# Hybrid decoder trunk on one core: another order of the twelve projection chunks, and the recurrence's side work one or two steps later

## The chip, the cores and the metric

The kernel runs on one core of a Trainium2 chip. The metric is the device time of one execution in microseconds, the median of several runs.

## What is computed

Two layers; each takes a residual `x` of 256 tokens by 1024 and adds the output projection of two mixers that share one input projection:

```python
def hybrid_layer(x, ...):
    h = rms_norm(x, norm_g)
    z = h @ w_in
    (rg_x, rg_gate, q, k_c, v_c, k_s, v_s, k_w, v_w, nsa_gate, br_gate) = jnp.split(z, cuts, axis=-1)
    y_a = rg_lru(causal_depthwise_conv(rg_x, conv_w, conv_b), ...)
    y_a = y_a * jax.nn.silu(rg_gate)
    y_b = nsa(q, k_c, v_c, k_s, v_s, k_w, v_w, br_gate, ...)
    y_b = y_b * jax.nn.silu(nsa_gate)
    return x + jnp.concatenate([y_a, y_b], axis=-1) @ w_out
def rg_lru(x, ...):
    r, i = sigmoid(x @ w_r + b_r), sigmoid(x @ w_i + b_i)      # eight blocks of 64
    a = exp(-8 r softplus(-lam))
    u = sqrt(1 - a * a) * (i * x)
    return associative_scan(h[t] = a[t] * h[t-1] + u[t])
```

`nsa` is an attention of eight query heads on two key heads with three branches: compressed blocks (a softmax over 15 compressed keys), selected blocks and a window; with 256 tokens the last two see the same causal keys.

## The kernel before

**Products.** Every weight is split into a high part `wh` and a remainder `wl` (float32 values of reduced width), and so is the normalised input (`hh`, `hl`). Each product is made of three matmuls, `mm3`, lines 172 to 175, on TensorE: L173, L174 and L175. The remainder of a weight chunk, L168, is made by VectorE; the high part by ScalarE (L165) or, for chunks marked `dma`, by a casting transfer that POOL issues (L156). The raw weights come over SP's queue (L148).

**Steps.** A layer is a list of steps; each has one weight chunk, and `plan` (from line 769) hangs side work on it. Eight steps project q and keys, five the compressed keys and the values. Then come **the twelve chunk steps that the change concerns**, numbered 0 to 11, each of 24 products of 256 columns (`fm`, L406) into a bank called `fm`, and eight steps of output projection (`out_proj`), numbered 12 and on in the plan. The chunks are of three kinds: `x0` to `x3` are the inputs of the recurrence (128 channels each), `g0` to `g3` its output gate, `n0` to `n3` the gate of the attention. What follows a chunk is

- `rg_x` (L640) behind an `x` chunk: one scaling L646 on VectorE into one of two `xpad` buffers, the convolution's first tap L647 on ScalarE, its other three L649 on VectorE; the result is `cx`;
- `silu_gate` (L540) behind every second `g` or `n` chunk, for the pair: L542 and L545 on VectorE, L544 on ScalarE; the result is `sgr` or `sgn`.

**Side work.** The table `SL` (line 53) says before which step each piece is issued: `gates` for `rg_gates` (L652: two gate products L657 on TensorE, then L660, L661, L663, L664 on ScalarE; for every second one L667, L670 on VectorE and L669 on ScalarE), `sqrt` for the root (L673, with a load of another activation table before it, and L674), `scan` for the recurrence's four scans (L678), `rout` for its output (L682, then L560 and L561 into `yy`, the operand of the output projection). The rest of the table is the attention: `qk` transposes queries and keys (L369, L378; `kd`, `kl`, `qs`: L373 to L383), `att` the scores of a head pair and a token half (L579 to L581 into one of three `s` banks, the maximum L584 or L586 on VectorE, the exponential L592 and the scaling L605 on ScalarE), `turn` their transposes (L618, copied by L83), `cmp` the compressed keys (L466, L470, L475 and so on), `cs` and `cpt` the compressed softmax (L509, L512, L515, L517 to L531, L536, and the copy `pct`, L83), `aout` the attention's output products (L628 to L634), which need `pct` and, right behind them on VectorE (L636), the gate `sgn`.

**What sets the order.** The steps are written out one after the other (lines 828 to 845). The tile framework then orders the instructions of each engine by its own estimate of the times and puts in the semaphores. On the chip each engine works its list off in that order: an instruction that waits holds up all that is behind it on the same engine. The weights are prefetched: loads run up to six steps ahead, in four raw buffers, casts up to five, and remainders one to three.

Of the kernel before, what the change touches and what calls it, by code (L numbers as in the profile page):

```python
# [38 lines left out]
for _n, _w in (("g", 8), ("cw", 16), ("cb", 4), ("br", 4), ("bi", 4), ("lam", 4)):  # L39
# [10 lines left out]
PRB = 6  # L50

K = dict(scale="A", ev1="A", hid="A", pct="A")
SL = dict(qk=(0, 2), order=("x0", "x1", "x2", "x3", "n0", "n1", "g0", "g1", "g2", "g3", "n2", "n3"),
          cmp=(2, 3, 4), att=(1, 3, 3, 4, 6, 7, 10, 11), turn=(2, 4, 5, 6, 8, 10,
          12, 13), cs=(5, 5), cpt=6, aout=(6, 7, 12, 15), gates=(2, 3, 4, 5), tab=6, sqrt=5,
          scan=8, rout=(9, 11))

# [12 lines left out]
def hybrid_trunk_kernel(ctx: ExitStack, tc: tile.TileContext, vx, wc, wt, wv, wf, wo, w1, w2, pe,  # L72
# [183 lines left out]
    def layer(l, prev):  # L256
# [4 lines left out]
        def step(chunk, run, after=None, before=(), middle=()):  # L261
            steps.append((chunk, run, after, before, middle))
# [502 lines left out]
        step(Chunk(wv[l, 0, :, 6:], 2, 280), R(tm2, 6, 2), v_out)  # L765
        order = [(o[0], int(o[1])) for o in SL["order"]]
        base = {"x": 0, "g": 4, "n": 8}
# [3 lines left out]
        def at(n, f, *a, mid=False):  # L771
            plan[n][1 if mid else 0].append(F(f, *a))

        at(1, cmp_hid)
        at(SL["qk"][0], qk_transpose, 0)
        at(SL["qk"][1], qk_transpose, 1)
        for n, f in zip(SL["cmp"], (cmp_act, cmp_kv, cmp_kt)):
            at(n, f)
        for q in range(8):
            i, t = divmod(q, 2)  # L780
            n = SL["att"][q]
            at(n, att_scores, i, t)
            at(n, att_coef, i, t, mid=True)
        at(SL["cs"][0], cmp_scores)
        at(SL["cpt"], cmp_pt)
# [168 lines left out]
```

## Time and profile before

| | us |
|---|---|
| median of three runs | 253.13 (252.58 to 253.38) |
| profiled execution, its own time | 252.82 |
| its span | 251.0 |
| twelve chunk steps of layer 0, from the first `fm` product to the output projection | 37.8 to 102 |
| the same of layer 1 | 158 to 222 |

| engine | busy us | share of the span |
|---|---|---|
| TensorE, matmuls | 243.0 | 97% |
| TensorE, weight loads | 222.2 | 88% |
| VectorE | 195.8 | 78% |
| ScalarE | 164.5 | 66% |
| POOL | 40.1 | 16% |

The busy share is an average over a span with several stages. Matmuls are pipelined, each shows some 0.28 us and the next begins 0.12 us after it, so a busy TensorE is not one at its peak. An instruction's length on VectorE and ScalarE overlaps the next by about 0.1 us; the pace of a queue is read from one start to the next.

### The profile page before, as it was taken

How to read it: one execution, taken by the hardware profiler on the slowest of the kernel's cores; microseconds unless marked ns; L12 is line 12 of the kernel's file. 1: busy time of each engine (PE TensorE's matmuls, PEld its weight loads, DVE VectorE, ACT ScalarE, POOL GpSimd, SP SyncE). 2: the span in 40 equal slices, each digit the busy share in tenths (PEclk: the TensorE clock that was granted, in tenths of full speed). 3: DMA queues.
4: the chain of work that ended last, by engine and by line, in shares of the span. 5: the costliest groups of instructions: out<-in, count | busy, mean ns of one | idle time of the engine just before them, and what ended most of it. 6: DMA issues, size and time to landing. Idle time of an engine off the chain costs nothing.

```text
span 251.0 us, 5217 instructions
## 1 busy us (share of the span) xinstructions
PE 243.0 (97%) x1958; PEld 222.2 (88%) x1958; DVE 195.8 (78%) x386; ACT 164.5 (66%) x419; POOL 40.1 (16%) x65
## 2 busy tenths in 40 slices
PE   7999998999999999999999999998999999999994
PEld 3989997977899798999999999996889879989993
DVE  4898798879999997654995569688999998765422
ACT  5966419799999967622873553849999996670000
POOL 0034460001811011000001044100100001010000
PEclk9999999999999999999999999999999999999999
DMA  6987999856699688562569878475249858833022
GB/s 211 371 289 226 318 413 407 265 168 202 195 322 403 184 266 293 174 202 72 167 207 347 312 236 263 159 230 187 93 167 347 317 177 268 271 127 84 3 84 84
DMA packets 17593, 57.17 MB, mean 228 GB/s; under 512 B 2208, under 2 KB 3360, under 8 KB 17056
## 3 DMA queue, kind: packets, MB, share of 16 engines
q1 hardware_dynamic: 12816, 39.86, 46.4%
q0 software_dynamic: 4608, 16.78, 20.9%
q8 instruction: 15, 0.25, 0.4%
q10 hardware_dynamic: 144, 0.20, 0.2%
q14 instruction: 10, 0.08, 0.1%
HBM read 55.78 MB, written 1.05 MB: 226 GB/s over the span
## 4 chain that ended last, share of the span: by engine, by line
PE 59%; DVE 19%; ACT 12%; DMA 4%; issue 2%; POOL 1%; SPq 0%; DVEq 0%; ACTq 0%
PE fm L173 11%; PE fm L175 10%; PE fm L174 10%; DVE wl L168 6%; PE s L174 4%; PE s L175 4%; PE s L173 4%; ACT pr L592 3%; PE m L628 3%; PE pp L618 3%; DMA raw<-in_wt_dram 2%; DMA raw<-in_wf_dram 2%; DVE cx L649 2%; POOL st L179 1%; DVE sm L584 1%
## 5 line engine op out<-in xcount | busy, mean ns | idle before, releaser
L168 DVE TENSOR_TENSOR wl<-raw,wh 128x1024 fp32r<-128x1024 f32 (+4 forms) x67 | 74.4, 1117 | 7.9 <-PE pp L174 3.0
L173 PE MATMUL fm<-hh,wh 128*128 128x256 f32 x192 | 56.9, 296 | 0.2
L174 PE MATMUL fm<-hl,wh 128*128 128x256 f32 x192 | 55.0, 287 | 0.0
L175 PE MATMUL fm<-hh,wl 128*128 128x256 f32 x192 | 54.5, 284 | 0.5 <-DVE wl L168 0.5
L165 ACT CAST wh<-raw 128x768 fp32r<-128x768 f32 (+4 forms) x35 | 30.8, 883 | 28.6 <-DMA raw<-in_wc_dram 7.6
L173 PEld LDWEIGHTS fm<-hh,wh 128*128 128x128 f32 x192 | 36.7, 191 | 2.1 <-issue 1.2
L175 PEld LDWEIGHTS fm<-hh,wl 128*128 128x128 f32 x192 | 36.7, 191 | 1.2 <-DVE wl L168 0.8
L174 PEld LDWEIGHTS fm<-hl,wh 128*128 128x128 f32 x192 | 36.7, 191 | 0.5 <-issue 0.4
L592 ACT ACTIVATE pr<-s,sm 128x128 f32<-128x128 f32 (+1 forms) x64 | 26.0, 417 | 9.4 <-DVE sm L586 6.0
L173 PE MATMUL fm<-yy,wh 128*128 128x256 f32 x96 | 27.4, 285 | 0.0
L175 PE MATMUL fm<-yy,wl 128*128 128x256 f32 x96 | 26.8, 279 | 0.0
L174 PE MATMUL fm<-yy,wh 128*128 128x256 f32 x96 | 26.8, 279 | 0.0
L605 ACT ACTIVATE pr<-pr,sm 128x128 f32<-128x128 f32 (+1 forms) x64 | 23.7, 455 | 1.8 <-DVE sm L598 1.8
L173 PEld LDWEIGHTS fm<-yy,wh 128*128 128x128 f32 x96 | 18.0, 188 | 1.5 <-DVE sm L597 0.8
L156 POOL DMA_DIRECT2D wh<-in_wo_dram x16 | 8.5, 530 | 66.2 <-PE fm L175 29.1
L174 PEld LDWEIGHTS fm<-yy,wh 128*128 128x128 f32 x96 | 18.1, 188 | 0.0
L175 PEld LDWEIGHTS fm<-yy,wl 128*128 128x128 f32 x96 | 18.0, 188 | 0.0
L174 PE MATMUL s<-wl,hh 128*128 128x384 f32 x48 | 16.5, 344 | 0.3 <-DVE wl L168 0.3
L723 DVE TENSOR_TENSOR head<-head,fm 128x512 f32<-128x512 f32 x11 | 7.5, 686 | 11.5 <-PE fm L175 11.5
L156 POOL DMA_DIRECT2D wh<-in_wf_dram x16 | 9.0, 565 | 46.2 <-PE fm L175 24.4
L175 PE MATMUL s<-wh,hl 128*128 128x384 f32 x48 | 16.2, 337 | 0.0
L173 PE MATMUL s<-wh,hh 128*128 128x384 f32 x48 | 15.6, 353 | 0.3 <-ACT wh L165 0.3
(205 smaller groups left out, 615.0 us busy)
## 6 DMA issues: line engine op xcount, KB each, us to landing
raw<-in_wf_dram SPq DMA_DIRECT2D x24, 512.0 KB, 4.5
wh<-in_wf_dram POOLq DMA_DIRECT2D x16, 512.0 KB, 4.8
raw<-in_wo_dram SPq DMA_DIRECT2D x16, 512.0 KB, 5.0
wh<-in_wo_dram POOLq DMA_DIRECT2D x16, 512.0 KB, 4.5
raw<-in_wt_dram SPq DMA_DIRECT2D x15, 384.0 KB, 3.9
yy<-in_w_dram SPq DMA_DIRECT2D x4, 1024.0 KB, 7.4
raw<-in_wc_dram SPq DMA_DIRECT2D x4, 512.0 KB, 5.2
raw<-in_wv_dram SPq DMA_DIRECT2D x4, 420.0 KB, 4.9
```

The source lines that it names most:

```text
L156: G.dma_start(self.wh, self.src)
L165: A.copy(hi[:, c], self.raw[:, c])
L168: V.tensor_tensor(lo[:, c], self.raw[:, c], hi[:, c].bitcast(F32), op=ALU.subtract)
L173: T.matmul(o, lh, rh, start=start, stop=False)
L174: T.matmul(o, lh, rl, start=False, stop=False)
L175: T.matmul(o, ll, rh, start=False, stop=stop)
L592: A.activation(pr[g][:, b], ov[:, b], AF.Exp, bias=sm[:, 0, 2 * g + b:2 * g + b + 1], accum_out=sm[:, 1, 2 * g + b:2 * g + b + 1])
L605: A.activation(pr[g][:, b], pr[g][:, b], AF.Copy, scale=sc_)
L618: T.transpose(pp[:, (2 * g + b) * P:(2 * g + b + 1) * P], pr[g][:, b, c * P:(c + 1) * P], ident)
L628: T.matmul(yb[g * HD:(g + 1) * HD, :S], L.vv[:, 0, b, g * HD:(g + 1) * HD], pt[:, g, b, 0:2].rearrange("p a s -> p (a s)"), start=(b == 0) ...
L649: V.scalar_tensor_tensor(cx[:, j], xp[:, 1 + k:1 + k + S], v(l, "cw", 4 * k + j), cx[:, j], op0=ALU.mult, op1=ALU.add)
L723: V.tensor_tensor(x_sb[:, m], x_sb[:, m], os_[0].rearrange("p (a s) -> p a s", a=2), op=ALU.add)
```

## The change

The chunks `n0` and `n1` go from steps 4 and 5 to steps 0 and 1; the four `x` chunks from steps 0 to 3 to steps 2 to 5; `g0` to `g3`, `n2` and `n3` stay. The gate products of the recurrence go from steps 2, 3, 4, 5 to steps 4, 5, 6, 7, its root from 5 to 7, its scan from 8 to 9, its output from 9 and 11 to 10 and 11. No instruction is added or removed.

```diff
-SL = dict(qk=(0, 2), order=("x0", "x1", "x2", "x3", "n0", "n1", "g0", "g1", "g2", "g3", "n2", "n3"),
+SL = dict(qk=(0, 2), order=("n0", "n1", "x0", "x1", "x2", "x3", "g0", "g1", "g2", "g3", "n2", "n3"),
           cmp=(2, 3, 4), att=(1, 3, 3, 4, 6, 7, 10, 11), turn=(2, 4, 5, 6, 8, 10,
-          12, 13), cs=(5, 5), cpt=6, aout=(6, 7, 12, 15), gates=(2, 3, 4, 5), tab=6, sqrt=5,
-          scan=8, rout=(9, 11))
+          12, 13), cs=(5, 5), cpt=6, aout=(6, 7, 12, 15), gates=(4, 5, 6, 7), tab=6, sqrt=7,
+          scan=9, rout=(10, 11))
```

How the instructions stand is shown at three places of layer 0.

VectorE, where the second input `cx` of the recurrence is finished (`xpad_72` is its scaled chunk; its last L649 is what the second gate product waits for). Before:

```order
L646 TENSOR_TENSOR xpad_72<-fm,rb 128x256
L598 TENSOR_TENSOR sm<-gate,sm 128x4
L375 TENSOR_TENSOR kl<-pp,kd_122 64x2x128
L649 SCALAR_TENSOR_TENSOR cx<-xpad_72,head,cx 128x256 x2
L375 TENSOR_TENSOR kl<-pp,kd_122 64x2x128
L649 SCALAR_TENSOR_TENSOR cx<-xpad_72,head,cx 128x256
```

With the change:

```order
L168 TENSOR_TENSOR wl<-raw,wh 128x1024
L646 TENSOR_TENSOR xpad_71<-fm,rb 128x256
L168 TENSOR_TENSOR wl<-raw,wh 128x1024
L649 SCALAR_TENSOR_TENSOR cx<-xpad_72,head,cx 128x256
L586 TENSOR_REDUCE sm<-s 128x4
L649 SCALAR_TENSOR_TENSOR cx<-xpad_72,head,cx 128x256
L597 RECIPROCAL sm<-sm 128x4
L168 TENSOR_TENSOR wl<-raw,wh 128x1024
L649 SCALAR_TENSOR_TENSOR cx<-xpad_72,head,cx 128x256
```

The three convolution taps of that input stood close together between small pieces of the key transposes; now weight remainders and score reductions stand before and between them.

TensorE, at the second gate product (L657; it reads `cx`). Before:

```order
L581 MATMUL s<-maskb,identb 128x2x128
L657 MATMUL fm<-cx,rws 128x256 x2
L579 MATMUL s<-kd_122,qs 128x512
L580 MATMUL s<-kl,qs 128x512
L581 LDWEIGHTS identb
```

With the change:

```order
L581 MATMUL s<-maskb,identb 128x2x128
L618 MATMUL pp<-cst,pr 128x128 x4
L657 MATMUL fm<-cx,rws 128x256
L515 MATMUL m<-cst,tmp 128x128 x2
L657 MATMUL fm<-cx,rws 128x256
L173 MATMUL fm<-hh,wh 128x256
```

The gate product stood between the scores of step 3; now it stands behind the scores of pair 2, and the transposes of the compressed softmax (L515) and the whole chunk `x3` are behind it.

ScalarE, around the copy `pct`, which the first output product of the attention needs. Before:

```order
L544 ACTIVATE sgn<-tmp_1045 128x512
L592 ACTIVATE pr,sm<-s,sm 128x128
L673 ACT_TABLE_LOAD
L673 ACTIVATE tl<-tl 128x1024
L83 COPY pct<-m 128x256
```

With the change:

```order
L83 COPY pt<-pp 128x4x128 x2
L660 ACTIVATE rr<-fm,hb 128x256
L661 ACTIVATE tmp_1078<-fm,hb 128x256
L663 ACTIVATE tl<-rr,sp 128x256
L83 COPY pct<-m 128x256
```

The gate `sgn`, the table load and the root stood ahead of the copy; now the third gate's activations do.

## Rows read from the trace of the kernel before

**Rows 1.** The page, part 1: busy time, share of the span, instructions.

```profile
PE 243.0 (97%) x1958; PEld 222.2 (88%) x1958; DVE 195.8 (78%) x386; ACT 164.5 (66%) x419; POOL 40.1 (16%) x65
```

**Rows 2.** Waits of TensorE: us in total, times, longest.

```profile
PE m L475 <- DVE hs L470: 0.8, 1, 0.8
PE pp L618 <- DVE kl L375: 0.8, 2, 0.5
PE fm L175 <- DVE wl L168: 0.5, 1, 0.5
...
PE s L579 <- ACT pr L592: 0.3, 1, 0.3
```

**Rows 3.** Stretches of layer 0: length, busy us (instructions) of PE, PEld, DVE, ACT, POOL, clock.

```profile
48.90:63.15 14.25, 13.45 (x90) 11.05 (x89) 11.96 (x33) 13.51 (x43) 1.69 (x3) 1.00 0.60 181
63.15:80.86 17.71, 17.71 (x146) 16.50 (x145) 17.64 (x33) 17.65 (x49) 6.76 (x11) 1.00 0.87 307
```

**Rows 4.** Timeline of TensorE, layer 0: start, length, instruction, wait before it.

```profile
48.91 1.03 PE L657 MATMUL fm<-cx,rws 128*128 128x256 f32 x4
49.58 0.47 PE L173 MATMUL fm<-hh,wh 128*128 128x256 f32 x1
...
52.59 0.63 PE L618 MATMUL pp<-cst,pr 128*128 128x128 f32 x4 [0.50 <-DVE kl L375]
...
56.38 0.36 PE L579 MATMUL s<-kd,qs 128*128 128x256 f32 x1
...
57.11 0.36 PE L173 MATMUL fm<-hh,wh 128*128 128x256 f32 x1
...
60.06 0.40 PE L579 MATMUL s<-kd,qs 128*128 128x512 f32 x1
...
66.98 0.64 PE L509 MATMUL m<-qT,kcb 128*32 128x256 f32 x8
...
80.86 0.65 PE L628 MATMUL m<-pt,vv 128*64 128x256 f32 x4
```

**Rows 5.** Timeline of VectorE, layer 0.

```profile
46.19 0.69 DVE L586 TENSOR_REDUCE sm<-s 128x4 f32<-128x512 f32 x1
...
50.98 1.00 DVE L649 SCALAR_TENSOR_TENSOR cx<-xpad,head,cx 128x256 f32<-128x256 f32 x2 [1.39 <-ACT cx L647]
...
55.57 1.23 DVE L168 TENSOR_TENSOR wl<-raw,wh 128x1024 fp32r<-128x1024 f32 x1
56.72 0.48 DVE L649 SCALAR_TENSOR_TENSOR cx<-xpad,head,cx 128x256 f32<-128x256 f32 x1
57.11 0.13 DVE L481 TENSOR_SCALAR ks__792<-ks__792 32x1 f32<-32x1 f32 x1
57.28 0.69 DVE L584 TENSOR_REDUCE sm<-s 128x2 f32<-128x512 f32 x1
57.89 0.48 DVE L649 SCALAR_TENSOR_TENSOR cx<-xpad,head,cx 128x256 f32<-128x256 f32 x1
```

**Rows 6.** Timeline of ScalarE, layer 0.

```profile
78.12 1.28 ACT L673 ACT_TABLE_LOAD   x1
...
80.38 0.36 ACT L83 COPY pct<-m 128x256 f32<-128x256 f32 x1
```

**Rows 7.** Timeline of VectorE, layer 1.

```profile
163.42 1.23 DVE L168 TENSOR_TENSOR wl<-raw,wh 128x1024 fp32r<-128x1024 f32 x1
...
166.60 0.69 DVE L586 TENSOR_REDUCE sm<-s 128x4 f32<-128x512 f32 x1
...
172.50 0.32 DVE L470 SCALAR_TENSOR_TENSOR hs<-hth,m 128x160 f32<-128x160 f32 x1
```

**Rows 8.** Timeline of TensorE, layer 1.

```profile
172.87 0.30 PE L475 MATMUL m<-w2s,hs 128*32 128x64 f32 x2 [0.82 <-DVE hs L470]
173.42 0.63 PE L618 MATMUL pp<-cst,pr 128*128 128x128 f32 x4 [0.25 <-DVE kl L375]
...
200.17 0.65 PE L628 MATMUL m<-pt,vv 128*64 128x256 f32 x4
```

## Prediction

> **What bounds the kernel now.** I read the busy shares first. TensorE (PE) is busy 97% of the span, its weight loads 88%, VectorE 78%, ScalarE 66% [rows 1]. That looks like a TensorE kernel, so next I asked where TensorE waits. In the chunk steps its waits come to 2.4 us for the whole program: 0.8 for `hs` (layer 1), 0.8 in two pieces for `kl`, 0.5 for the first chunk's remainder `wl` (which the change does not touch), 0.3 for a score bank that ScalarE still reads [rows 2]. By their times all lie in the first five of the twelve steps, so an order of chunks can gain about 1.9 us there and no more. Third, the section cut in two stretches for layer 0 [rows 3]. From 48.90 to 63.15 VectorE is busy 11.96 of 14.25 us. From 63.15 to 80.86 it is busy 17.64 of 17.71 and ScalarE 17.65: both are full to the brim, and TensorE is full too, without one visible wait. **So the early steps have idle time on VectorE, and the middle steps have none on three engines.** That is the picture that the change has to be laid on.
>
> **The change, part by part.** Nothing is added or removed on any engine: the twelve chunks have the same shape, and the gates, root, scan and outputs of the recurrence are the same instructions. Two things move.
>
> *The two attention-gate chunks first.* In steps 0 and 1 VectorE and ScalarE lose the recurrence's first two inputs (per input one L646 and three L649 on VectorE, at a L649's pace of 0.39 us each [rows 5], and one L647 on ScalarE) and get one pair of gate operations (L542, L545, L544). All four inputs, 4 x 4 x 0.39 = 6.2 us of VectorE, now come after the third chunk, that is, after about 53 us in layer 0; before, half of it was done by then. Its cover was the idle time of the early stretch, 14.25 - 11.96 = 2.3 us. That cover is used less now, and the work goes to the stretch that has 0.07 us left.
>
> *The gates two steps later.* A gate product occupies TensorE from 48.91 to 49.58, 0.67 us [rows 4]. Before the softmax product L509 at 66.98 TensorE ran three of them; now it runs one there. TensorE does no less in all, but it reaches every point in the middle 1.34 us earlier, while VectorE does not.
>
> **Layer 0, walked along the queues.** Step 2: the transposes L618 wait for `kl` today (0.50 at 52.59 [rows 4]). `kl` hangs on a ScalarE chain that begins with the reduction L586 at 46.19 [rows 5]; the change takes one L649 from in front of L586 but puts the next weight remainder (L168, 1.15 us [rows 5]) there, so L586 stays within 0.2 us. TensorE comes with 23 products ahead of L618 instead of a gate and 18, which is 0.1 us less. This wait stays: no gain.
>
> The new wait is at the second gate product. TensorE: L509 comes at 66.98 - 1.34 - 0.12 (one score product that is no longer ahead) = 65.5. Then come L509 itself (0.57), the scores of pair 2 for both token halves (0.73 for the short half, as 56.38 to 57.11 [rows 4]; the long half has twice the columns but the same number of instructions, so between 0.73 and 1.46: I take 1.2) and four transposes (0.4): it stands before the gate product at about 68.4. Its operand is the second input's last L649. VectorE: the first reduction of the 512-wide scores now sits right behind the first L646 and can end at about 55.0 (L618 at 52.2, its 0.4, four products and the two of L475/L476 to 54.3, then 0.6). Behind it, up to that L649, the order has five L168 (55.57 to 56.72 [rows 5]: 5 x 1.15 = 5.75), six L649 and two L646 (8 x 0.39 = 3.1), seven operations on 512 columns (57.28 to 57.89 [rows 5]: 7 x 0.6 = 4.2) and thirteen small ones (0.1 each, below the L481 there: 1.3): 14.35 us, so 69.35, and 0.15 for the moments at which VectorE waits for ScalarE (1.39 us such a wait took once in step 2 before [rows 5]): **69.5. TensorE waits about 1.1 us.** Queued behind that product on TensorE are the softmax transposes L515 and the whole fourth input chunk, so nothing fills the hole.
>
> From there to the first output product of the attention (L628), TensorE has a gate, L515, two chunks (2.95 each, as 57.11 to 60.06 [rows 4]), eight transposes, a gate and L536: 9.2 us, to 78.7. VectorE needs, from 69.5, 7.0 us of queue to L531 and waits about 1 us for ScalarE's exponential in between: 77.5; L536 and then the copy `pct`, which stands behind three gate activations on ScalarE, end at about 79.0. The two come out nearly together; I take 79.0. Today L628 starts at 80.86 [rows 4], but with 23 more chunk products (2.8) and one more gate (0.67) ahead of it, which now follow it: 80.86 - 3.5 = 77.4 would be its place with today's waits. **Layer 0 loses 79.0 - 77.4 = 1.6 us.** Behind L628 I see no new wait: the scan, the root and both table loads (1.28 us, now behind `pct`, no longer ahead of it [rows 6]) have steps 8 to 11 to run in, where the products alone are 4 x 2.95 us, and the recurrence's last output is wanted only by the output projection.
>
> **Layer 1.** Here the front does gain. L586 runs at 166.60, behind two L168 (from 163.42) and two L649 [rows 7]; without the L649, and with the L168 from about 163.0, since no L646 stands ahead of them, it starts at 165.3, 1.3 us earlier. ScalarE then reaches `hs` earlier, and VectorE ends L470 at about 171.7 instead of 172.8 [rows 7]; TensorE, which has no gate product there, waits until 171.7. Before, L475 started at 172.87, with 0.67 us of gate behind it [rows 8]: 172.87 - 0.67 - 171.7 = 0.5 gained, and the 0.25 us before L618 [rows 8] as well. The middle takes it back by the same count as in layer 0: the third gate's operand is at about 192.4 for a TensorE that is there at 191.75 (0.65), the fourth costs 0.25, and `pct` lands at 199.0 for a L628 whose place, with ten chunk products moved behind it, is level with 200.4 against 200.17 [rows 8]. **Layer 1 loses 0.2 us.**
>
> **Edits at nothing.** POOL issues the same weight loads in the same order. On SP one output-weight load goes ahead of the small load of the gate weights of layer 1; those are wanted a chunk section later, so it costs nothing. The clock stays: it was granted in full in both stretches, the early one with 0.8 us of TensorE idle in it included [rows 3].
>
> **The sum** against the profiled execution's own 252.82 us: +1.6 + 0.2 = **254.6 us**. The median of the three runs, 253.13, is 0.3 above that execution; I leave this in the range. Bounds: in layer 0 both of today's waits could go (-0.8), or the smaller ones that I fold into the walk (a gate's bank, 0.4; the score bank of pair 2, 0.9) could add to it (+2.9). In layer 1, -1.1 (all its waits go) to +1.6 (it behaves as layer 0).
>
> **The rivals.**
>
> *No change, 253.1.* TensorE has the work and the waits only change place. The Trainium skill ("Perfetto Trace Analysis", Identifying the Most-Contended Engine) says to work on the engine with the highest occupancy, and that for TensorE matmul busy time does not measure headroom while weight-load time does. By its first half alone an edit that leaves TensorE's work alone would leave the time at 253.1. For this rival: 97% busy, and waits of 1.9 us in all. Against it: in the middle of layer 0 VectorE (17.64) and ScalarE (17.65) are above TensorE's weight loads (16.50) [rows 3], so there the fullest engine is another.
>
> *Faster, 251.5.* The front's relief shows in both layers (0.75 in layer 1, up to 0.8 in layer 0) and the middle does not take it back. It decides at one place: VectorE has to finish the second input 1.1 us before my 69.5. That happens if the L168 of later chunks do not run ahead of it, or if the small operations cost less than I booked. For it: ScalarE has two table loads and the root (2.3 us from 78.12 to 80.38 [rows 6]) less ahead of `pct`. Against it: the order puts a L168 between the second and third L649.
>
> *Slower in both layers, 256.5.* Layer 1 pays as layer 0 does, 2 x 1.6 and some of the smaller waits. Against it: in layer 1 the scheduler puts the gate product in the midst of the scores, and the front gains.
>
> That the change does nothing is excluded: the order on three engines differs.
>
> **Chances.** Forecast 0.40, slower in both layers 0.18, no change 0.20, faster 0.22. A run of this kernel can tell some 0.3%, 0.76 us, from no change. So faster 0.22, same 0.20, slower 0.58. The range leaves a tenth at either end: from 252.0, half way into the faster case, to 256.3, short of the worst.
>
> **What would show it.** Right: a wait of TensorE at L657 on VectorE's `cx` of about 1 us near 69 us in layer 0; VectorE idle for longer between 47 and 55 us; L586 of layer 1 near 165.3; waits of TensorE in the section of layer 0 above 2 us, in layer 1 near 1.3. Wrong: no wait at L657, or L628 of layer 0 before 78 us; then the faster case holds. If waits appear after L628, in steps 8 to 11, my claim that the moved scan and root are covered is wrong.

## The result, and the profile after the change

| | before | after |
|---|---|---|
| median | 252.86 us (252.22 to 253.38) | 255.83 us (255.67 to 256.35) |
| span of the profiled execution | 251.0 | 254.2 |
| twelve chunk steps of layer 0, first `fm` product to first product of the output projection | 64.06 | 67.39 |
| the same of layer 1 | 63.84 | 64.09 |

The change makes the kernel slower: the ratio is 1.0126, with a 95% interval from 1.0105 to 1.0146, so 3.0 us. The 3.2 us of the spans lie almost wholly in one place: layer 0's chunk steps +3.33, layer 1's +0.25, the program ahead of them -0.45, the rest +0.07. Times are compared between runs at the full granted clock; the profiled execution of one experiment, e7, ran at 0.56 of it (394.8 us) and is left out.

The busy times hardly move. Part 1 of the page after, against [rows 1]:

```profile
PE 243.8 (96%) x1958; PEld 221.8 (87%) x1958; DVE 196.1 (77%) x386; ACT 165.1 (65%) x419; POOL 39.5 (16%) x65
```

The waits of TensorE do. In the same form as [rows 2] (us in total, times, longest):

```profile
PE fm L657 <- DVE cx L649: 1.6, 2, 1.0
PE pp L618 <- DVE kl L375: 1.3, 1, 1.3
PE m L475 <- DVE hs L470: 1.2, 1, 1.2
...
PE fm L173 <- ACT tmp L661: 0.3, 1, 0.3
...
PE s L579 <- ACT pr L592: 0.2, 1, 0.2
```

There is a wait at the gate product L657 that was not there, and those for `kl` and `hs` are longer in total. The listed waits of layer 0's section come to 2.8 us, against 1.35 before, so they hold less than half of the 3.33; the rest stands in delays that the list has in part or not at all. TensorE in layer 0, where [rows 4] stood:

```profile
52.38 0.63 PE L618 MATMUL pp<-cst,pr 128*128 128x128 f32 x4 [1.26 <-DVE kl L375]
...
65.68 0.64 PE L509 MATMUL m<-qT,kcb 128*32 128x256 f32 x8
...
67.41 0.50 PE L579 MATMUL s<-kd,qs 128*128 128x512 f32 x1 [0.17 <-ACT pr L592]
...
70.65 0.70 PE L657 MATMUL fm<-cx,rws 128*128 128x256 f32 x2 [1.04 <-DVE cx L649]
...
79.93 0.65 PE L628 MATMUL m<-pt,vv 128*64 128x256 f32 x4
```

The wait at L618 is 1.26 (0.50 before), that at the second gate product 1.04. L628 starts 0.9 us earlier than before, but a whole chunk (24 products) and a gate, some 3.5 us, now follow it instead of standing ahead of it. VectorE at the same time, where [rows 5] stood:

```profile
46.33 0.69 DVE L586 TENSOR_REDUCE sm<-s 128x4 f32<-128x512 f32 x1
47.49 0.69 DVE L542 TENSOR_TENSOR tmp<-fm,rb 128x512 f32<-128x512 f32 x1 [0.47 <-PE fm L175]
48.59 0.18 DVE L597 RECIPROCAL sm<-sm 128x4 f32<-128x4 f32 x1 [0.41 <-ACT pr L592]
...
49.87 0.69 DVE L545 SCALAR_TENSOR_TENSOR sgn<-sgn,tmp 128x512 f32<-128x512 f32 x1 [0.24 <-ACT sgn L544]
51.81 0.43 DVE L375 TENSOR_TENSOR kl<-pp,kd 64x256 fp32r<-64x256 f32 x1 [1.25 <-ACT kd L374]
...
54.62 0.69 DVE L584 TENSOR_REDUCE sm<-s 128x2 f32<-128x512 f32 x1 [0.84 <-PE s L581]
...
69.01 1.19 DVE L168 TENSOR_TENSOR wl<-raw,wh 128x1024 fp32r<-128x1024 f32 x1
70.12 0.47 DVE L649 SCALAR_TENSOR_TENSOR cx<-xpad,head,cx 128x256 f32<-128x256 f32 x1
```

The last row is the third convolution tap of the second input, for which L657 waits; a weight remainder stands right ahead of it. The first six rows show where VectorE lost its time: from 47 to 55 us it waits again and again, mostly for ScalarE. Two stretches of 18 us, the first from about the start of the section, show it as a sum. Columns as in [rows 3]; before the change:

```profile
37.40:55.40 18.00, 16.80 (x174) 14.90 (x173) 15.04 (x29) 16.41 (x43) 1.62 (x3) 1.00 0.84 293
55.40:73.40 18.00, 17.70 (x133) 15.30 (x133) 17.91 (x39) 17.37 (x56) 7.38 (x12) 1.00 0.71 217
```

And after it:

```profile
37.40:55.40 18.00, 16.63 (x176) 14.84 (x176) 12.41 (x22) 14.84 (x40) 1.62 (x3) 1.00 0.89 299
55.40:73.40 18.00, 16.40 (x113) 12.87 (x112) 17.51 (x41) 15.39 (x50) 7.72 (x11) 1.00 0.64 199
```

**In the first 18 us VectorE (third pair of numbers) does 12.41 us of work instead of 15.04. In the next 18 it is full both times, and there TensorE loses 1.3 us of busy time (17.70 to 16.40).** The 2.6 us of work that VectorE did not do in front are still to be done behind. The clock was granted in full in all four stretches.

Layer 1, VectorE and TensorE, where [rows 7] and [rows 8] stood. The section starts 2.87 us later than before:

```profile
168.37 0.69 DVE L586 TENSOR_REDUCE sm<-s 128x4 f32<-128x512 f32 x1
...
172.94 0.69 DVE L545 SCALAR_TENSOR_TENSOR sgn<-sgn,tmp 128x512 f32<-128x512 f32 x1 [1.33 <-ACT sgn L544]
...
174.89 0.32 DVE L470 SCALAR_TENSOR_TENSOR hs<-hth,m 128x160 f32<-128x160 f32 x1
```

```profile
175.27 0.30 PE L475 MATMUL m<-w2s,hs 128*32 128x64 f32 x2 [1.22 <-DVE hs L470]
...
195.86 0.92 PE L657 MATMUL fm<-cx,rws 128*128 128x256 f32 x3 [0.56 <-DVE cx L649]
```

L586 is 1.1 us earlier than before (168.37 - 2.87 = 165.50 against 166.60), but behind it VectorE waits 1.33 us for the attention gate's tangent (L544 on ScalarE), and L475 gains nothing: it starts at 172.40 of the old time, and the old start, 172.87, less the 0.67 us of the gate product that no longer stands ahead of it would be 172.20.

### The profile page after: what moved, and what is told of

Read it like the earlier page. It is cut to its first block, busy times and chain, and to the rows that moved or that the text cites. A ratio compares the mean times of both kernels' runs of the same rounds, so it can differ in the third digit from the quotient of the medians.

```text
span 254.2 us, 5220 instructions
## 1 busy us (share of the span) xinstructions
PE 243.8 (96%) x1958; PEld 221.8 (87%) x1958; DVE 196.1 (77%) x386; ACT 165.1 (65%) x419; POOL 39.5 (16%) x65
## 4 chain that ended last, share of the span: by engine, by line
PE 63%; ACT 13%; DVE 13%; DMA 6%; issue 3%; SPq 0%; DVEq 0%; ACTq 0%
PE fm L173 11%; PE fm L174 11%; PE fm L175 11%; DVE wl L168 6%; DMA raw<-in_wf_dram 4%; PE s L174 4%; PE s L175 4%; PE s L173 4%; ACT pr L592 3%; PE m L628 3%; PE pp L618 3%; ACT pr L605 3%; PE fm L657 2%; DMA raw<-in_wt_dram 2%; DVE cx L649 2%
## 5 line engine op out<-in xcount | busy, mean ns | idle before, releaser
L168 DVE TENSOR_TENSOR wl<-raw,wh 128x1024 fp32r<-128x1024 f32 (+4 forms) x67 | 74.2, 1116 | 7.2 <-PE pp L174 2.8
L592 ACT ACTIVATE pr<-s,sm 128x128 f32<-128x128 f32 (+1 forms) x64 | 26.6, 430 | 9.1 <-DVE sm L584 4.8
L605 ACT ACTIVATE pr<-pr,sm 128x128 f32<-128x128 f32 (+1 forms) x64 | 24.5, 467 | 1.6 <-DVE sm L598 1.6
L83 ACT COPY pt<-pp 128x512 f32<-128x512 f32 x24 | 13.6, 602 | 6.4 <-PE pp L618 6.4
```

What stands on the lines that cost most here:

```text
L83: A.copy(o, i)
L168: V.tensor_tensor(lo[:, c], self.raw[:, c], hi[:, c].bitcast(F32), op=ALU.subtract)
L592: A.activation(pr[g][:, b], ov[:, b], AF.Exp, bias=sm[:, 0, 2 * g + b:2 * g + b + 1], accum_out=sm[:, 1, 2 * g + b:2 * g + b + 1])
L605: A.activation(pr[g][:, b], pr[g][:, b], AF.Copy, scale=sc_)
```

## The experiments

All of them, in the order in which they are told. "Section" is the length of the twelve chunk steps in the profiled execution. In e4_taps_after, e10 and e12 the remainder of the very first chunk of layer 0 came 1.0 to 1.3 us late (0.5 in the kernel before, not at all in the changed one); this lies in the section of layer 0, and differences of a microsecond there are read with it in mind. The kernel before was run again beside each group of experiments, with medians from 252.45 to 252.75 us, and each experiment's ratio is to those runs. The profiled executions of e8 and e12 (257.49 and 253.15 us) were the longest of their runs, so their sections are long as well.

| run | median us | ratio to before (95%) | section, layer 0 | layer 1 |
|---|---|---|---|---|
| changed kernel | 255.83 | 1.0126 (1.0105 to 1.0146) | 67.39 | 64.09 |
| e2_side | 256.99 | 1.0173 (1.0151 to 1.0194) | 66.58 | 65.62 |
| e8_scan_early | 256.47 | 1.0154 (1.0133 to 1.0176) | 67.14 | 64.63 |
| e4_taps_after | 252.54 | 1.0007 (0.9989 to 1.0026) | 65.03 | 63.33 |
| e4_taps_before | 252.38 | 0.9993 (0.9976 to 1.0009) | 64.19 | 63.50 |
| e5_gates8 | 255.56 | 1.0128 (1.0103 to 1.0153) | 65.89 | 65.10 |
| e9_gates8_l509 | 254.44 | 1.0065 (1.0048 to 1.0083) | 65.52 | 63.69 |
| e6_second_gate | 254.96 | 1.0104 (1.0071 to 1.0137) | 66.21 | 63.84 |
| e7_no_ahead | 255.42 | 1.0107 (1.0088 to 1.0125) | - | - |
| e11_scores_new | 252.97 | 1.0018 (0.9997 to 1.0038) | 64.27 | 63.82 |
| e10_scores_old | 252.31 | 0.9989 (0.9970 to 1.0008) | 65.02 | 63.54 |
| e13_remainders_front | 252.76 | 1.0018 (0.9993 to 1.0043) | 63.52 | 64.02 |
| e12_scores_gates | 251.70 | 0.9953 (0.9930 to 0.9976) | 64.34 | 62.84 |

### Is it the order of the chunks, or the later side work?

The old order with the new places of the side work:

```diff
-SL = dict(... order=("n0", "n1", "x0", "x1", "x2", "x3", ...
+SL = dict(... order=("x0", "x1", "x2", "x3", "n0", "n1", ...
```

> The old order of chunks with the new places of the side work (gates in steps 4 to 7, root 7, scan 9, outputs 10 and 11). If the order of the chunks costs the time (my theory): between 252.3 and 253.5 us, no wait at L657, and the waits at L618 and at the remainder as before. If the later side work costs it: 255.0 to 256.0, with waits of TensorE after the first L628 of a layer or at the output projection. If both share it: about 254.3.

Measured 256.99 us, slower than any theory had it, and slower than the whole change. The two stalls that cost most are alike in both layers. TensorE and, at the same time, VectorE in layer 0 of this run:

```profile
72.90 1.07 PE L657 MATMUL fm<-cx,rws 128*128 128x256 f32 x4
75.32 0.36 PE L173 MATMUL fm<-hh,wh 128*128 128x256 f32 x1 [1.35 <-issue]
```

```profile
74.22 0.41 DVE L524 TENSOR_REDUCE m<-sc 128x16 f32<-128x256 f32 x1
74.54 0.68 DVE L542 TENSOR_TENSOR tmp<-fm,rb 128x512 f32<-128x512 f32 x1
```

Behind a gate product the next chunk product has to wait for a bank `fm`, of which there are two. One holds the gates, the other the pair `n0`/`n1` that VectorE reads with L542; that one stood behind reductions and the softmax in VectorE's queue and ended at 75.2, and the chunk starts at 75.32 (in layer 1: L542 from 196.32 to 197.0, chunk at 197.10). The profile names no releaser there; the cause is read from these times. So late gates are no cheap edit in the old order. What follows for the changed kernel: its loss is not the sum of two independent edits (the new order with earlier gates was not run), and "the order costs it, the late gates don't" is wrong as I had it.

The other half of the question, the scan and the outputs alone put back:

```diff
-          scan=9, rout=(10, 11))
+          scan=8, rout=(9, 11))
```

> The changed kernel with the scan in step 8 and the outputs of the recurrence in steps 9 and 11 again, as before the change; order of chunks, gates and root stay changed. My theory (these pieces are covered by four steps of products): 255.3 to 256.3 us, no difference. If the later scan and outputs cost part of the 3 us: 255.0 or less.

Measured 256.47, a little above the range, and no gain: nothing is to be had by putting the scan and the outputs back, as the prediction said.

### Is it VectorE's work?

Two of the three taps that VectorE adds to each input are left out, in both kernels:

```diff
-            for k in range(3):
+            for k in range(1):
                 V.scalar_tensor_tensor(cx[:, j], ...
```

> The changed kernel without two of the three convolution taps that VectorE adds to each input of the recurrence (two L649 of three left out, 8 per layer, 8 x 0.39 = 3.1 us of VectorE per layer). My theory (VectorE is late for the second gate product): four of them lie ahead of that product, 1.56 us, so the wait at L657 goes: 254.0 to 254.7 us. If what costs the time is the chunk order at the front (the wait for kl at L618) or the later side work: 255.4 to 256.0.

> The kernel before without the same two taps. My theory: no product of TensorE waited for an L649 there, so 252.6 to 253.3 us; the difference to the changed kernel without them falls from 3.0 to under 2 us. If VectorE's load in the middle sets the time in both: 251.0 to 252.0, and the difference stays near 3.

Measured 252.54 and 252.38: 3.3 us less than the changed kernel (3.0 by the ratios), nothing that can be told from zero in the kernel before. No difference between the two can be told any more, where I had expected it only to fall below 2 us. **The work that could be left out of the old order without gain is what the new order pays for.** TensorE's wait at L657 is no longer among its waits. One reserve: in the old order without the taps the waits for `kl` came to 2.4 us, against 0.8 with them, so a gain may be hidden there.

### Is it the wait at the second gate product?

All gates one step later:

```diff
-          ... gates=(4, 5, 6, 7), tab=6, sqrt=7,
+          ... gates=(5, 6, 7, 8), tab=6, sqrt=8,
```

> The changed kernel with the four gate products one step later again (steps 5 to 8, root 8). My theory: the wait of TensorE at the second gate product (1.04 us shown, some 1.3 with what the modelled end hides) goes, since its operand comes at 70.5 us and TensorE gets there at about 72.5; the wait at L618 (1.26) stays: 254.3 to 255.0 us. If VectorE as a whole is what is late in the middle of layer 0, the wait only moves to the next operand (the compressed softmax and its copy, L515 or L628): 255.5 to 256.2. If the lateness of the side work costs the time: above 256.2.

Measured 255.56, above my range and not to be told from the changed kernel, but the sections can: layer 0 gained 1.50 us (67.39 to 65.89), and layer 1 lost 1.01. The loss is in eight small matmuls. L509 in layer 1 of this run:

```profile
184.00 0.62 PE L509 MATMUL m<-qT,kcb 128*32 128x256 f32 x2
184.55 0.66 PE L618 MATMUL pp<-cst,pr 128*128 128x128 f32 x4
185.13 0.63 PE L509 MATMUL m<-qT,kcb 128*32 128x256 f32 x4
185.69 0.44 PE L618 MATMUL pp<-cst,pr 128*128 128x128 f32 x2
186.06 0.62 PE L509 MATMUL m<-qT,kcb 128*32 128x256 f32 x2
```

From the start of each group to the next instruction it is 0.55 us, whether the group has two or four; after the last, L657 starts at 186.61. The eight cost 1.66 us; together they cost 0.57 in the changed kernel (187.28 to 187.85). The next run puts them together again:

```diff
-          ... cs=(5, 5), cpt=6, aout=(6, 7, 12, 15), gates=(4, 5, 6, 7), tab=6, sqrt=7,
+          ... cs=(4, 4), cpt=6, aout=(6, 7, 12, 15), gates=(5, 6, 7, 8), tab=6, sqrt=8,
```

> The changed kernel with all gates one step later (5 to 8), as in the run before, and the scores of the compressed softmax issued in step 4, so that the eight products L509 stand together again. In the run before they were split into groups of 2 and 6 (layer 0) and 2, 4, 2 (layer 1), each group took about 0.55 us, and L509 cost 1.11 and 1.66 us where it cost 0.57 together. If that split is what took back the gain: 255.56 - 0.54 - 1.09 = 253.9, between 253.4 and 254.5 us. If it is an accident of the records: 255.2 to 256.0. If the softmax comes too early for its operands: a wait of TensorE at L509 or L497.

Measured 254.44, inside the range, with L509 in one piece in both layers:

```profile
64.09 0.64 PE L509 MATMUL m<-qT,kcb 128*32 128x256 f32 x8
...
184.01 0.64 PE L509 MATMUL m<-qT,kcb 128*32 128x256 f32 x8
```

Layer 1 went from 65.10 to 63.69. In layer 0 the second gate product no longer waits for its operand, yet it starts only at 73.07, some 0.7 us behind the usual pace. The eight transposes L618 ahead of it (from 71.49) come in pairs 0.4 us apart, as the weight loads of three pairs wait 0.20 us each for ScalarE's scaling L605, and the gate's own weight load waits 0.19 for the fourth input's L646 (72.61 to 73.02), which frees a bank `fm`. So later gates take the one wait away, worth 1.5 to 1.9 us of layer 0's 3.3, and the lateness of ScalarE and VectorE shows again at the next places. A second way to the same place, with three gates later and the first where it was:

```diff
-          ... gates=(4, 5, 6, 7), tab=6, sqrt=7,
+          ... gates=(4, 6, 7, 8), tab=6, sqrt=8,
```

> The changed kernel with the first gate product where it is and the other three one step later (steps 4, 6, 7, 8, root 8). The eight small products L509 stay together, and behind them comes a whole chunk (2.95 us) before the second gate product. My theory: TensorE reaches that product about 3 us later, after its operand (70.5 us), so the wait there goes, 1.2 us in layer 0, and the 0.6 us at the third gate of layer 1: 253.6 to 254.6 us. If VectorE is late with everything in the middle, the wait only moves to the compressed softmax (L515) or to the first output product (L628): 255.3 to 256.2.

Measured 254.96, 0.4 above the range; its interval overlaps with the changed kernel's. The section of layer 0 is 1.18 shorter, that of layer 1 0.25, and no wait at L657 is left. One of 0.3 for a bank `fm` (for L646) is new, and that of some 0.35 for L661, which the changed kernel has too, stayed. The third way leaves the gates and changes VectorE's queue:

```diff
 def ahead(n):
-    return 0 if n < 4 else 1 if n < 7 else ...
+    return 0 if n < 4 or 15 <= n < 19 else 1 if n < 7 else ...
```

> The changed kernel, but in layer 0 the remainders of four chunks are made one step later, not a step ahead of need. Between the first and the last convolution tap of the second input VectorE then has two remainders fewer in its queue (2 x 1.15 = 2.3 us). My theory: the operand of the second gate product comes about 2.3 us earlier, its wait goes, and 1.0 to 1.3 us are gained: 254.4 to 255.0, unless the remainders themselves come late for their chunks. In that case waits for wl of up to a microsecond show on TensorE, and it is 255.3 to 256.3. If the order in VectorE's queue does not matter: 255.6 to 256.0 without any wait for wl.

Measured 255.42, above the range of my theory. There is no profile of it that can be read beside the others, so whether the wait went and one for `wl` came stays open; the median says only that nothing was gained that can be measured.

### Is it the front?

The first block of scores one step later, in the changed kernel:

```diff
-          cmp=(2, 3, 4), att=(1, 3, 3, 4, 6, 7, 10, 11), turn=(2, 4, 5, 6, 8, 10,
+          cmp=(2, 3, 4), att=(2, 3, 3, 4, 6, 7, 10, 11), turn=(3, 4, 5, 6, 8, 10,
```

> The changed kernel with the same first block of scores one step later. The front gains: the waits at L618 of layer 0 (1.26) and at L475 of layer 1 (1.2) go. My theory: TensorE then comes to the second gate product earlier still and VectorE does not, so most of it turns into a longer wait there: 254.4 to 255.6 us, L657 waiting 1.5 to 2.5 us in layer 0. If the two waits at the front were what the change costs: 253.0 to 253.8.

Measured 252.97, level with the kernel before. My expectation was wrong by 1.4 us, and the reason is instructive. The list of waits looks at first as I had said:

```profile
PE fm L657 <- DVE cx L649: 2.3, 2, 1.2
```

But these are one wait of 1.16 us in each layer, at the third gate product (72.64 and 192.53). The second gate product, which I meant, starts at 64.85 us in layer 0 without a wait. I had assumed that VectorE comes no earlier. It does. The first two stretches of this run and two of its key copies:

```profile
37.40:55.40 18.00, 17.62 (x186) 15.80 (x185) 14.92 (x27) 14.56 (x41) 2.33 (x4) 1.00 0.92 315
55.40:73.40 18.00, 16.84 (x126) 14.44 (x125) 17.07 (x39) 17.03 (x53) 5.86 (x12) 1.00 0.78 250
```

```profile
47.61 0.42 DVE L375 TENSOR_TENSOR kl<-pp,kd 64x256 fp32r<-64x256 f32 x1 [0.30 <-ACT kd L374]
...
49.70 0.43 DVE L375 TENSOR_TENSOR kl<-pp,kd 64x256 fp32r<-64x256 f32 x1
```

The last `kl` copy starts at 49.70 instead of 51.81 and waits for nothing, since four exponentials and four scalings no longer stand ahead of ScalarE's key copies, and VectorE works 14.92 us in the first stretch instead of 12.41. The third tap of the second input ends 6.3 us earlier, counted from the start of the section (26.96 against 33.22). The number lies at the edge of the other case that I had set down, that the two waits at the front are the cost (253.0 to 253.8), but the sections speak against it: layer 0 gained 3.12 us, where the wait at L618 was 1.26, and layer 1, where the 1.2 us for `hs` went, gained 0.27. The same edit in the kernel before:

> The kernel before with its first block of scores one step later (step 2 instead of 1, its transposes in step 3), which takes four exponentials and four scalings, 2.8 us of ScalarE, out of the queue ahead of the second key copies. My theory: the waits for kl (0.8 in all) and hs (0.8) go: 251.2 to 252.4 us. If the middle of the layer takes the gain back: 252.5 to 253.3.

Measured 252.31; no difference that can be told. The waits for `kl` and `hs` went as I had said, and 1.2 us at L628 (for `tmp`, L636), 0.5 at L579 and 0.8 more for the first chunk's remainder came. VectorE did more in the first stretch here too, 16.19 us against 15.04, and nothing came of it:

```profile
37.40:55.40 18.00, 16.53 (x172) 14.38 (x170) 16.19 (x30) 14.77 (x37) 1.62 (x3) 1.00 0.88 288
```

That leaves two readings: ScalarE's queue as such, or VectorE's idle time. The last experiment touches VectorE's order alone: it lets the remainders of four chunks, which the program holds behind the query and key copies, be made in the gaps.

```diff
-            if n in (2, 3, 4, 5):
+            if n in ():
                 c.after = (lambda t: lambda: L.qk_done[t])(0 if n < 4 else 1)
```

> The changed kernel; the only edit is that the remainders of the third to sixth chunk are no longer held back behind the query and key copies, so that VectorE can make them in the idle time of the front. In the first 18 us of the section of layer 0 VectorE is busy 15.0 us before the change, 12.4 with it, 14.9 and 15.1 in the two runs with the later block of scores. If this idle time is what the change costs (my theory now): VectorE is busy 14 us or more there, the second input is finished some 2 us earlier, L657 waits less than 0.5 us, and it is 253.4 to 254.8 us. If the remainders push the key copies back: the wait at L618 grows beyond 1.5 us and it is 255.3 to 256.5. If the front of VectorE has nothing to do with it and the block of scores matters for ScalarE alone: 255.4 to 256.2 with L657 waiting about 1 us as in the changed kernel.

Measured 252.76, below the range that my theory gave it, level with the kernel before. Its stretches, VectorE at the place of the gap, and its waits:

```profile
37.40:55.40 18.00, 17.87 (x189) 16.06 (x188) 17.06 (x30) 15.44 (x43) 2.19 (x4) 1.00 1.04 383
55.40:73.40 18.00, 17.57 (x128) 14.77 (x128) 15.14 (x38) 16.34 (x53) 7.92 (x11) 1.00 0.68 209
```

```profile
50.04 0.32 DVE L470 SCALAR_TENSOR_TENSOR hs<-hth,m 128x160 f32<-128x160 f32 x1
50.28 1.22 DVE L168 TENSOR_TENSOR wl<-raw,wh 128x1024 fp32r<-128x1024 f32 x1
51.41 0.68 DVE L545 SCALAR_TENSOR_TENSOR sgn<-sgn,tmp 128x512 f32<-128x512 f32 x1
52.13 0.43 DVE L375 TENSOR_TENSOR kl<-pp,kd 64x256 fp32r<-64x256 f32 x1
```

```profile
PE fm L657 <- DVE cx L649: 1.1, 2, 0.7
...
PE pp L618 <- DVE kl L375: 0.5, 1, 0.5
```

What is left at L657 is 1.1 us in both layers together (I had said under 0.5), at the third gate product; in layer 0 it is 0.43. VectorE is busy 17.06 of the first 18 us, with a remainder where it used to wait for the key copy; the copy is only 0.3 us later than in the changed kernel. The third tap of the second input ends 28.29 us after the section's start (33.22), and the section of layer 0 takes 63.52 us, 3.87 less. **So what the change costs is VectorE's lost time in the front of layer 0, whose work then stands ahead of the recurrence's second input.** Three quite different edits give it back and all end level with the kernel before: less VectorE work (1.0007), the gap's cause moved away (1.0018), the gap filled (1.0018). Two reserves: the framework re-plans the lists of all engines for each edit, so that TensorE's order differs a little too, and its part isn't separated. And a full front is not enough: e2 has 14.91 us of VectorE in the first stretch and is the slowest of all, with 2.7 us of waits that I read as waits for the banks.

### The later scores and the later gates together

Both edits in the changed kernel:

```diff
-          cmp=(2, 3, 4), att=(1, 3, 3, 4, 6, 7, 10, 11), turn=(2, 4, 5, 6, 8, 10,
-          12, 13), cs=(5, 5), cpt=6, aout=(6, 7, 12, 15), gates=(4, 5, 6, 7), tab=6, sqrt=7,
+          cmp=(2, 3, 4), att=(2, 3, 3, 4, 6, 7, 10, 11), turn=(3, 4, 5, 6, 8, 10,
+          12, 13), cs=(5, 5), cpt=6, aout=(6, 7, 12, 15), gates=(5, 6, 7, 8), tab=6, sqrt=8,
```

> The changed kernel with both: the first block of scores one step later, and the gates one step later (5 to 8, root 8); the eight products L509 stand together. My theory: neither wait is left, 255.83 - 1.2 (gate) - 1.2 (kl) - 1.2 (hs) = 252.2, between 251.4 and 253.2 us, so this order of chunks is then no worse than the one before. If the middle of layer 0 is short of VectorE as a whole: 253.8 to 255.0, with TensorE waiting at L515, L536 or L628 instead.

Measured 251.70, 0.47% below the kernel before (0.24 to 0.70%). No wait for `kl`, `hs` or `cx` is left in either layer; what TensorE still waits for in the chunk steps is the first chunk's remainder, 1.0 us. The released remainders of e13 were not tried on top of it, nor the two edits together in the old order.

## Why the prediction was right, and where it was not

**The sign and the place: right.** 254.6 was forecast, in a range of 252.0 to 256.3, and 255.83 came. The cover that the prediction named, VectorE's idle time in the early stretch, is what decided, and the new wait stands at the second gate product, on VectorE's third tap, with a remainder ahead of it. VectorE idle for longer between 47 and 55 us, over 2 us of waits in layer 0's section, no new wait in steps 8 to 11: all seen. In layer 1 the waits came to 1.8 us, not 1.3.

**The size in layer 0: +1.6 forecast, +3.3 measured.** The step that was sized too small is VectorE's way to that tap. It was put at 14.35 us of queue from 55.0, plus 0.15 for moments of waiting. The reduction L584 ended at 55.31 and the tap at 70.59, so the way took 15.3 us, of which 0.42 was one wait for ScalarE (L597, at 63.24). The section began 0.45 earlier than before; by its own time the reduction was 0.8 us late and the tap 1.5. TensorE came to the gate 1.5 us late by the same reckoning (at 69.4 us of its run, where 68.4 was forecast), because the score banks came late (0.7 us ahead of the two L579 at 67.41 and 68.31, of the 0.9 that had been folded away) and the wait at L618, which was to stay at 0.50, took 1.26; some 0.5 of that is no new loss, as the wait for the first chunk's remainder did not come in this run. So the wait at the gate, 1.04 shown, looked like the forecast 1.1 by luck, two errors of one size. From the gate to L628 the walk held (9.5 us forecast, 9.28 measured).

The deeper fault is in the method. The idle time of the front was counted (14.25 - 11.96 = 2.3 us), "that cover is used less now" was said, and then the loss was built from TensorE's waits one by one. The plain account of VectorE, 2.6 us less done in front while it is full behind, gives nearly the whole of the 3.0 at once here; e2 and e10 show that it doesn't hold for every edit.

**Layer 1: +0.2 forecast, +0.25 measured, partly by luck.** L586 came at 165.50 of before's time, as said (165.3). But `hs` let TensorE go at 172.40 of that time instead of 171.7, because the gate's L545 stood ahead on VectorE and waited for ScalarE: nothing was gained in front. The third gate's wait (0.65 forecast, 0.56 shown) came, the fourth's 0.25 did not.

**The rivals.** "No change" leaned on the Trainium skill ("Perfetto Trace Analysis", Identifying the Most-Contended Engine): to work on the fullest engine. TensorE's busy time moved by 0.8 us, its weight loads by 0.4, and the time by 3.0; what cost it was an engine that is 77% busy over the whole span and full in one stretch. The "faster" rival named the right condition, that the second input be finished earlier because remainders do not stand ahead of it: e13 made it so, and the loss went, though no gain over the kernel before came of it. "Slower in both layers" did not happen.

**Side work.** That scan and outputs are covered held (e8; the root and the table loads were not put back by themselves). That the gates' later place costs only through `cx` did not hold in general: e2 shows that it can cost more through the two `fm` banks.

## What to carry to other kernels

Where an engine is idle in one stretch and full in the next, work that used to fill the first can cost its whole length when it is moved: count that engine's busy time per stretch before and after the move, and not only the waits of the engine it feeds. More work in front than before is worth nothing by itself: 16.19 us in the old order (e10) and 17.06 in the new one (e13) came out level with the 15.04 of the kernel before. A gap of the kind can be closed from three sides (less work, the cause of the gap moved, other work let into it), and hints that hold work back for the sake of one copy should be tried again whenever the order around them changes. Gains in front count only if the next wait is taken away too: the later scores alone brought the new order level with the old one, and with the later gates it came out 0.47% ahead.

## What the runs showed of the hardware that I had not expected

The eight matmul records of L509 (four products in the program) on 128 x 32 tiles cost 0.57 us together and 1.66 when transposes split them in groups of 2, 4 and 2: each group pays some 0.55 whatever its number. The Trainium skill ("TensorEngine Tiling (Array Packing)", Key Properties) says that a change of tiling mode drains TensorE; these rows fit that, but they would also fit products of one group that run side by side, and no run separates the two.

Some of VectorE's operations were longer beside POOL's table products (L245 to L250). In the changed kernel the remainder L168 at 66.12 took 1.35 us and the tap L649 at 67.40 took 0.61, where 1.22 and 0.47 are usual; two other remainders beside those products, at 64.58 and 69.01, took 1.22 and 1.19. The Trainium skill ("SBUF — State Buffer", Who interferes with whom) says that a VectorE instruction with two SBUF inputs contends with a GpSimd instruction that reads SBUF; two of these four rows agree, and it is a small part (0.3 us) of the queue that had been sized too short.
